# Block sums kept from the second normalisation, the search closed two units sooner, the bias kept on the chip, and low queries loaded once

## The chip, the cores and the metric

The kernel runs on one core of a Trainium2 chip. The metric is the device time of one execution in microseconds. The core has five engines that work side by side: TensorE (PE, matmuls, with its weight loads shown as PEld), VectorE (DVE), ScalarE (ACT), GpSimd (POOL) and SyncE (SP), which here only issues transfers (DMA). Each engine takes its instructions in one fixed order; a wait at the head of an engine's list holds everything behind it.

## The reference

One layer of an encoder on x of 2048 rows and 1024 columns, all in float32:

```python
xn = rms_norm(h, norm_gain[layer])
proj = xn @ w_in[layer]
qa, ka, va, ga, qb, kb, vb, gb, iq, ik, iw, za, zb = jnp.split(proj, offsets, axis=-1)
ya = chunked_relpos_attention(qa, ka, va, rel_bias[layer]) * jax.nn.silu(ga)
...
yb = dsa_sparse_attention(qb, kb, vb, iq, ik, iw) * jax.nn.silu(gb)
merged = sigmoid(za + b0) * (yA @ w_branch_a) + sigmoid(zb + b1) * (yB @ w_branch_b)
h = h + merged @ w_out[layer]
return rms_norm(h, final_norm_gain)
```

Branch A has 8 heads of 64; each chunk of 64 queries sees its own chunk and the 8 before, with a bias `rel_bias[h, clip(dist, -256, 256) + 256]`. For keys more than 256 rows back the distance is clipped, so the bias there is one number per head. Branch B scores all keys with an indexer (`iq`, `ik`, `iw`), takes the 256 best per query and attends to those.

## The kernel before

**Numbers.** A float32 operand is held as a high and a low part (`xh`, `xl`; weights likewise), both of the type fp32r; a product is three matmuls: high·high, high·low, low·high (`mm3`, L213). In the attention, `qs` holds the queries' high part on 128 rows (twice) and the low part on 128 rows (twice), and `kk` holds the keys' high part on rows 0–63 and low part on rows 64–127, so that two matmuls give all four products.

**Groups and slots.** x is cut into four groups g of 512 rows. Two slots of x are resident. First g=0 and 1 are projected; then `norm_again` (L1177) loads x of g=3 and 2 again, normalises and splits it (`split_x`: L225 on DVE, L226 on ACT, L227 on DVE) into the two slots.

**Jobs.** The projection is a list of jobs, each a unit of 256 columns by one group (two chunks of 24 matmuls 128x512; a `va` unit four chunks of 128x288). Jobs 0–39 do all units for g=0, 1. Jobs 40–43 are `va` for g=3 and 2, jobs 44–55 are the units of `rest` for g=3 and 2, in the order zb, za, qb. The other units of g=3 and 2 are done as 12 "quads": a Winograd scheme on 2x2 blocks, with 7 block products (84 matmuls) where 8 would be usual. Its inputs are the blocks A11, A12 (slot of one group, halves of the depth), A21, A22 and four block sums: A11 − A21 (stored over A21), S2, S1 and S4. `combine` (L1196) makes one sum for one k: POOL adds the high parts (L1203), DVE the low ones (L1204), DVE joins both (L1205), ACT rounds the high part (L1206), DVE takes the rest (L1207). It runs 16 times: four times behind the last g=3 job (`turned`), twelve times while the first quads run. The quads' weights come by `prep_full` (tiles `wst` from `wS`, combined on POOL at L1227–1233, split by L1236 and L1237).

**The search.** The top-k threshold search is written as generators that run between chunks: after each chunk `tick` lets DVE work worth `PUMP` or `PUMP2` be written. When all is written, `close_search` (L750) runs `search_again`: a matmul (L577) counts rows where the search failed, DVE turns the count into a flag (L579), and each engine passes a branch (for a slower search that isn't needed here). Behind the branch the search's buffers are given back, and the pools of the quads and of the attention are opened.

**The attention.** For each head and group, `load_a` (L835) loads `qs` (four transfers of 128 KB), `kk`, `vs` (the values, out of `vA`, in pieces of 512 B) and the bias tile of 640 columns, prepared for each head by `bias_half` (L659) during jobs 10–25. `a_unit` makes scores (L878) in two segments of 320 keys, or one where fewer than 640 are seen, and `softmax_piece` (L809) adds the bias.

The instructions are put in order by a scheduler when the program is built, so what follows what on an engine is read from the built program.

Of the kernel before, what the change touches and what calls it, by code (L numbers as in the profile page):

```python
# [8 lines left out]
F32 = mybir.dt.float32  # L9
# [31 lines left out]
PUMP, PUMP2 = 4500, 5400  # L41
# [12 lines left out]
CTB, WSB = 2, 5  # L54
# [38 lines left out]
def block_kernel(ctx: ExitStack, tc: tile.TileContext, io, dbg=None):  # L93
# [18 lines left out]
    vA = [scratch(f"vA{g}", [512, H, 2, HD]) for g in range(NG)]  # L112
# [11 lines left out]
    biasD = [scratch(f"biasD{h}", [128, 640]) for h in range(H)]  # L124
# [534 lines left out]
    def bias_half(j, gate):  # L659

        h, half = j // 2, j % 2
        c_ = slice(half * 320, half * 320 + 320)
        bt = ev.tile([128, 320], F32, name="bt", tag="ef")
        nc.gpsimd.tensor_copy(bt[:, 0:1], gate)
        nc.sync.dma_start(bt, io["bias"][h][:, c_])
        nc.gpsimd.tensor_scalar(bt, bt, -1.0, None, op0=OP.mult)
        if half:
            nc.gpsimd.memset(bt[0:64, 256:320], FAR)
        else:
            nc.gpsimd.memset(bt[64:128, 0:64], FAR)  # L670
        nc.sync.dma_start(biasD[h][:, c_], bt)
# [44 lines left out]
    def evac_v(c, g, o, acc):  # L716
        vv = ev.tile([128, 2, 32], F32R, name="vvt", tag="ef") if early_ else evl.tile([128, 2, 32], F32R, name="vv", tag="vv")
        nc.scalar.activation(vv[:, 0], acc[:, 256:288], AF.Copy)
        nc.vector.tensor_tensor(vv[:, 1], acc[:, 256:288], f32(vv[:, 0]), op=OP.subtract)  # L719
# [6 lines left out]
        nc.sync.dma_start(vA[g][o * 128:(o + 1) * 128, c * 4:c * 4 + 4], f32(e))  # L726
# [7 lines left out]
    rest = [u for k in ("zb", "za", "gb", "ga", "qb", "ka", "qa") for u in left[k]]  # L734
# [13 lines left out]
    dn = att = ldb = wp2 = ld = sml = wk = wy = wz = dna = wp_ = pl_ps = pe = psd = kBt = vBt = mk01 = None  # L748

    def close_search():  # L750

        nonlocal ld
        early_.append(1)
        stage.pop()
        search_again()
        search_st.close()
        ld = dph.enter_context(pool("ld", bufs=2, side="right"))

# [11 lines left out]
    def open_late():  # L770
        nonlocal dn, att, ldb, wp2, pl_ps, psd, kBt, vBt, mk01
        late.append(1)
        dn = dph.enter_context(pool("dn", bufs=2))
        att = ph.enter_context(pool("att"))
        ldb = ph.enter_context(pool("ldb", bufs=2))
        wp2 = ph.enter_context(pool("wp2"))
        pl_ps = dph.enter_context(pool("pl_ps", space=PSUM))
        psd = dph.enter_context(pool("psd", space=PSUM))
        kBt = att.tile([128, 2, S], F32R, name="kBt")
        vBt = att.tile([128, NT, 128], F32R, name="vBt")  # L780
        mk01 = att.tile([128, 2, 256], BF16, name="mk01")
# [53 lines left out]
    def load_a(G, h):  # L835
        base = max(0, 4 * G - 4)
        q = ld.tile([128, 2, 512], F32R, name="qs", tag="qs")
        for hl in range(2):
            for half in range(2):
                nc.sync.dma_start(f32(q[half * 64:half * 64 + 64, hl, :]), qA[G][hl, :, h, :])  # L840
        kk = ld.tile([128, 1024], F32R, name="kk", tag="kk")
        v = ld.tile([128, 8, 128], F32R, name="vs", tag="vs")
        for i, g in enumerate(range(max(0, G - 1), G + 1)):
            nc.sync.dma_start(f32(kk[:, i * 512:i * 512 + 512]), kA[g].rearrange("l r h n -> (l r) h n")[:, h, :])
            nc.sync.dma_start(f32(v[:, 4 * i:4 * i + 4]), vA[g][:, h].rearrange("(t p) l d -> p t (l d)", p=128))
        bias = ld.tile([128, 640], F32, name="bias", tag="bias")
        nc.sync.dma_start(bias, biasD[h])
        return base, q, kk, v, bias

    def a_unit(G, h):  # L850
        st = {}

        def loads():
            st["ld"] = load_a(G, h)
            if h % 2 == 0:
                sg = ld.tile([128, 512], F32, name="sg", tag="sg", bufs=SGB)
                nc.sync.dma_start(sg, gAD[G][(h // 2) * 128:(h // 2) * 128 + 128])
                shared["sg", "a", h // 2] = sg

        def one():  # L860
            base, q, kk, v, bias = st["ld"]
# [7 lines left out]
            for j in range(4):  # L869
                i = 4 * G + j  # L870
                f = max(0, i - 4)
                nk = (i - f + 1) * 128
                segs = [(0, 320), (320, 320)] if nk == 640 else [(0, nk)]
                for a, w in segs:
                    s_ps = next_s()
                    ko = (f - base) * 128 + a
                    for m in range(2):
                        nc.tensor.matmul(s_ps[:, :w], q[:, m, j * 128:(j + 1) * 128], kk[:, ko:ko + w],  # L878
                                         start=(m == 0), stop=(m == 1))
                    softmax_piece(s_ps[:, :w], bias[:, 640 - nk + a:640 - nk + a + w], a == 0,  # L880
                                  P[:, j, a:a + w], mx[:, j:j + 1])
                    yield
                nc.scalar.activation(P[:, j, :nk], P[:, j, :nk], AF.Exp, bias=mx[:, j:j + 1], scale=-1.0,  # L883
                                     accum_out=sm[:, h % 2, j:j + 1])

        def two():
            base, q, kk, v, bias = st["ld"]
# [257 lines left out]
    def attention():  # L1145
        units[1][0]()
# [49 lines left out]
    def combine(dst, a, b, op, k):  # L1196

        (ah, al), (bh, bl), (dh, dl) = a(k), b(k), dst(k)
        if early_:
            t, t2 = (mid.tile([128, 512], F32, name="ct", tag="wst", bufs=WSB) for _ in range(2))  # L1200
        else:
            t, t2 = (evl.tile([128, 512], F32, name="ct", tag="ct", bufs=CTB) for _ in range(2))
        nc.gpsimd.tensor_tensor(t, f32(ah), f32(bh), op=op)  # L1203
        nc.vector.tensor_tensor(t2, f32(al), f32(bl), op=op)  # L1204
        nc.vector.tensor_tensor(t, t, t2, op=OP.add)  # L1205
        nc.scalar.activation(dh, t, AF.Copy)  # L1206
        nc.vector.tensor_tensor(dl, t, f32(dh), op=OP.subtract)  # L1207
# [31 lines left out]
    for i, (how, r_, u, g) in enumerate(jobs):  # L1239
# [4 lines left out]
        for c in range(4 if kind == "va" else 2):  # L1244
            acc = next_acc(i)
            if kind == "va":
# [4 lines left out]
                for _ in range(1):  # L1251
                    if again:
                        again.pop(0)()
                tick(0.5)
            else:
# [23 lines left out]
    close_search()  # L1279
    mid_st = ExitStack()  # L1280
    mid = mid_st.enter_context(pool("mid", side="right"))
    sums_ = {n: [mid.tile([128, 4, 512], F32R, name=f"{n}{z}") for z in "hl"] for n in ("s4", "s1", "s2")}
# [29 lines left out]
    def rest_of(q):  # L1312
# [3 lines left out]
        for z, x_ in enumerate((S2, S1, S4)):  # L1316
# [7 lines left out]
    prep_full(0, "V")  # L1324
    prep_full(1)
    turns = [lambda k=k: combine(S2, A22, A21, OP.subtract, k) for k in range(4)]
    turns += [lambda k=k, f=f: f(k) for k in range(4) for f in (lambda k: combine(S1, S2, A11, OP.add, k),
                                                                lambda k: combine(S4, A12, S2, OP.subtract, k))]
    ahead = first(0)
    for _ in ahead:  # L1330
        turns.pop(0)()
    for q in range(nq):
# [4 lines left out]
        if turns:  # L1337
            for _ in nxt:
                while turns[:1]:
                    turns.pop(0)()  # L1340
# [149 lines left out]
```

## Time and profile before

| | |
|---|---|
| median of 3 runs | 2124.75 us (2120.24 to 2125.8) |
| profiled execution, device time | 2117.65 us |
| its span in the trace | 2115.9 us |
| granted PE clock, mean | 0.982 |
| PE busy | 2011.0 us (95%) |
| DVE busy | 1477.2 us (70%) |

The stages in the profiled execution, by their places in the trace: first norm and indexer to 120 us; jobs for g=0 and 1, with the search beside them, to about 610; normalising again and `va` to about 690; the `rest` jobs to 820; the quads to about 1096; the attention and the output projection to the end. A row of the table of stretches has the start and end, the length, then for PE, PEld, DVE, ACT and POOL the busy time and the instructions, then PE's granted clock (1.00 is full), the share of the DMA engines' time and GB/s. In a row of the timeline the bracket tells how long the engine stood before it, and what it waited for.

### The profile page before, as it was taken

The page shows a single profiled execution, that of the slowest core. Times are in us where ns is not written, and L with a number is a line of the kernel's source. Part 1 is how long each engine was busy: PE and PEld are TensorE (multiplying, and loading weights), DVE is VectorE, ACT ScalarE, POOL GpSimd, SP SyncE. Part 2 cuts the span into 40 slices and gives each one's busy share as a digit, 9 for nine tenths or more (in the row PEclk, how much of TensorE's full clock was granted, in tenths as well). Part 3 has the DMA queues.
Part 4 walks back from the last instruction along what each step waited for, and adds up shares of the span by engine and source line. Part 5 has one row for each costly group of instructions (what it writes and reads, how often), then busy time and mean ns, then how long its engine had stood idle before and what let it go on. Part 6 is the DMA issues. An engine that isn't in the chain of part 4 may idle for free.

```text
span 2115.9 us, 33695 instructions
## 1 busy us (share of the span) xinstructions
PE 2011.0 (95%) x10714; PEld 1699.1 (80%) x10714; DVE 1477.2 (70%) x3728; ACT 1264.9 (60%) x2590; POOL 777.5 (37%) x953
## 2 busy tenths in 40 slices
PE   8799999999989998799988999999999999999998
PEld 7578888889878886478766888888888888887886
DVE  5748887969789645966536677866886688875444
ACT  5456575555555623365437778967896688873221
POOL 2122223321131223655414556446444543442420
PEclk9899999999999999899999999999999999999999
DMA  9473344454463423234468766467445742145642
GB/s 358 140 227 128 122 154 154 133 197 133 160 207 97 149 88 128 70 106 144 130 206 246 215 198 195 138 190 235 119 136 175 228 130 63 60 132 181 217 144 90
DMA packets 236806, 334.29 MB, mean 158 GB/s; under 512 B 29264, under 2 KB 115664, under 8 KB 236496
## 3 DMA queue, kind: packets, MB, share of 16 engines
q1 hardware_dynamic: 236624, 332.10, 49.1%
q8 instruction: 85, 1.39, 0.3%
q14 instruction: 97, 0.79, 0.1%
HBM read 225.62 MB, written 106.40 MB: 157 GB/s over the span
## 4 chain that ended last, share of the span: by engine, by line
PE 46%; DMA 4%; DVE 4%; ACT 2%; issue 2%; POOL 1%; SPq 0%; DVEq 0%; ACTq 0%; POOLq 0%
PE acc L213 8%; PE po L1385 8%; PE d L213 7%; PE O L1013 5%; PE s L988 5%; PE pt L1005 5%; PE O L923 3%; PE s L878 2%; PE pt L913 2%; DMA dst<-wB 1%; DMA wst<-wS 1%; DVE P L809 1%; DMA dst<-wA 1%; DVE ct L1205 1%; DVE ct L1204 1%
## 5 line engine op out<-in xcount | busy, mean ns | idle before, releaser
L213 PE MATMUL acc<-xh,wt 128*128 128x512 f32 x1920 | 622.4, 396 | 16.9 <-ACT wt L1236 8.6
L213 PEld LDWEIGHTS acc<-xh,wt 128*128 128x128 f32 x1920 | 361.3, 189 | 102.5 <-ACT wt L1236 10.0
L213 PE MATMUL acc<-xl,wt 128*128 128x512 f32 x960 | 378.4, 394 | 0.0
L205 POOL TENSOR_TENSOR wt<-wst,wt 128x512 fp32r<-128x512 f32 (+1 forms) x116 | 149.5, 1317 | 406.3 <-ACT wt L204 376.9
L830 POOL TENSOR_TENSOR ptl<-pf,pth 128x512 fp32r<-128x512 f32 (+1 forms) x144 | 179.6, 1247 | 216.7 <-ACT pf L826 145.0
L833 DVE TENSOR_TENSOR ptl<-pt,pth 128x512 fp32r<-128x512 f32 (+1 forms) x288 | 187.3, 660 | 48.1 <-ACT pth L832 47.0
L213 PEld LDWEIGHTS acc<-xl,wt 128*128 128x128 f32 x960 | 181.7, 189 | 40.0
L482 DVE SCALAR_TENSOR_TENSOR sc<-lg,iw,sc 128x512 f32<-128x512 f32 (+2 forms) x266 | 179.1, 678 | 41.2 <-ACT lg L477 37.0
L477 ACT ACTIVATE lg<-lg 128x512 f32<-128x512 f32 (+2 forms) x304 | 150.2, 523 | 69.7 <-PE lg L475 68.0
L988 PE MATMUL s<-kBt,qsB 128*128 128x512 f32 (+3 forms) x640 | 187.7, 382 | 0.7 <-DVE mx L809 0.5
L832 ACT ACTIVATE pth<-pt 128x512 fp32r<-128x512 f32 (+1 forms) x288 | 160.9, 579 | 24.4 <-PE pt L1005 11.5
L1005 PE MATMUL pt<-ident,P 128*128 128x128 f32 x1088 | 165.6, 273 | 1.9 <-DVE ptl L833 0.8
L991 ACT ACTIVATE P<-P,mx 128x128 f32<-128x128 f32 (+15 forms) x128 | 154.6, 1209 | 15.4 <-DVE mx L809 14.8
L809 DVE CUSTOM_DVE_ANT_0 P<-s,mk,mx 128x512 f32<-128x512 f32 (+2 forms) x192 | 125.1, 652 | 35.3 <-PE s L988 29.2
L1013 PE MATMUL O<-pth,vBt 128*128 128x256 f32 x544 | 147.3, 289 | 2.0 <-DVE yb L1023 1.4
L1013 PE MATMUL O<-ptl,vBt 128*128 128x256 f32 x544 | 145.9, 295 | 1.6 <-POOL ptl L830 1.1
L1005 PEld LDWEIGHTS pt<-ident,P 128*128 128x128 f32 x1088 | 127.7, 140 | 10.9 <-ACT pf L826 2.1
L1051 POOL TENSOR_TENSOR dw<-dst,dw 128x512 fp32r<-128x512 f32 x64 | 83.3, 1301 | 126.6 <-ACT dw L1050 108.3
L878 PE MATMUL s<-kk,qs 128*128 128x320 f32 (+1 forms) x448 | 108.8, 338 | 15.3 <-DMA kk<-kA 9.3
L213 PE MATMUL acc<-wt,xh 128*128 128x288 f32 x512 | 107.6, 304 | 7.7 <-DVE vv L719 4.8
L988 PEld LDWEIGHTS s<-kBt,qsB 128*128 128x128 f32 x640 | 102.5, 189 | 13.8 <-DVE mx L809 6.6
L883 ACT ACTIVATE P<-P,mx 128x640 f32<-128x640 f32 (+4 forms) x128 | 98.0, 768 | 24.4 <-DVE mx L809 23.9
(287 smaller groups left out, 4603.3 us busy)
## 6 DMA issues: line engine op xcount, KB each, us to landing
wst<-wP SPq DMA_DIRECT2D x108, 256.0 KB
qs<-qA SPq DMA_DIRECT2D x128, 128.0 KB
kk<-kA SPq DMA_DIRECT2D x56, 256.0 KB
vs<-vA SPq DMA_DIRECT2D x56, 256.0 KB
wst<-wS SPq DMA_DIRECT2D x52, 256.0 KB
bias<-biasD SPq DMA_DIRECT2D x32, 320.0 KB
xrow<-x SPq DMA_DIRECT2D x16, 512.0 KB
sBD<-ef SPq DMA_DIRECT2D x32, 256.0 KB
```

The lines of the kernel that those rows point to most:

```text
L213: nc.tensor.matmul(acc, a, b, start=(first and i == 0), stop=(last and i == n - 1), **({} if first and last else {"skip_group_check": True}))
L477: nc.scalar.activation(lg, lg, AF.Relu)
L482: nc.vector.scalar_tensor_tensor(o_, lg, wv, o_, op0=OP.mult, op1=OP.add)
L830: nc.gpsimd.tensor_tensor(lo, pf, f32(hi), op=OP.subtract)
L832: nc.scalar.activation(hi, src, AF.Copy)
L833: nc.vector.tensor_tensor(lo, src, f32(hi), op=OP.subtract)
L878: nc.tensor.matmul(s_ps[:, :w], q[:, m, j * 128:(j + 1) * 128], kk[:, ko:ko + w], start=(m == 0), stop=(m == 1))
L988: nc.tensor.matmul(s_ps[:, :w], q[:, h, :], kBt[:, m, a:a + w], start=(m == 0), stop=(m == 1))
L991: nc.scalar.activation(P[:, e, :n], P[:, e, :n], AF.Exp, bias=mx[:, e:e + 1], scale=-1.0, accum_out=st["sum"][:, (u % 2) * 2 + e:(u % 2) * ...
L1005: nc.tensor.transpose(pt[:, k, e, :], P[:, e, (kt + k) * 128:(kt + k + 1) * 128], ident)
L1013: nc.tensor.matmul(o_, vBt[:, kt + k, :], src[:, k, :], start=(kt + k == 0 and n_ == 0), stop=(kt + k == b and n_ == 1), skip_group_check= ...
L1385: nc.tensor.matmul(accs[t, hf], a, b[:, n_], start=(k == 0 and i == 0), stop=(k == KT - 1 and i == 2))
```

## The change

1. **Block sums.** `norm_again` takes blocks k and k+4 together. For g=3 the normalised x is stored (`xnD`); for g=2 it is read back (`xa`), POOL makes all four sums in float32 with four operations, and two transfers store them (`sumD`). Later `load_sum` loads each sum and splits it with one ACT and one DVE operation. `combine` is gone. While such parts are pending, fewer are taken per chunk and `tick` is halved.
2. **The search's close.** `rest` begins with qb; `PUMP2` is 6900; `tick` itself calls `close_search` once the search is written. It opens three more accumulators (`psw`), and loads the sums.
3. **The bias.** `load_bias` loads 384 columns per head once (`bres`) and prepares them on POOL; five heads at the close, three when the attention opens. Beyond 384 keys the bias is a tile of zeros with the mask (`bfar`), as the constant of the head is taken off. Segments are 256 + 384 keys; 512 keys are 128 + 384.
4. **Low queries once.** `qs` takes three transfers instead of four, and the low part is multiplied on 64 rows (the product low·low is dropped).
5. **`vA`** is laid out so that a head's values for a group are one contiguous 2 KB row per partition; **`wst`** has 4 buffers instead of 5.

```diff
-PUMP, PUMP2 = 4500, 5400
+PUMP, PUMP2 = 4500, 6900
-CTB, WSB = 2, 5
+WSB, NB = 4, 5
...
-    def bias_half(j, gate):
-
-        h, half = j // 2, j % 2
-        c_ = slice(half * 320, half * 320 + 320)
-        bt = ev.tile([128, 320], F32, name="bt", tag="ef")
-        nc.gpsimd.tensor_copy(bt[:, 0:1], gate)
-        nc.sync.dma_start(bt, io["bias"][h][:, c_])
-        nc.gpsimd.tensor_scalar(bt, bt, -1.0, None, op0=OP.mult)
-        if half:
-            nc.gpsimd.memset(bt[0:64, 256:320], FAR)
-        else:
-            nc.gpsimd.memset(bt[64:128, 0:64], FAR)
-        nc.sync.dma_start(biasD[h][:, c_], bt)
+    def load_bias(heads, pl):
+
+        for h in heads:
+            bres[h] = pl.tile([128, 384], F32, name=f"bres{h}")
+            nc.sync.dma_start(bres[h], io["bias"][h][:, 256:640])
+        for h in heads:
+            c_ = pl.tile([128, 1], F32, name=f"bcol{h}")
+            nc.gpsimd.tensor_copy(c_, bres[h][:, 0:1])
+            nc.gpsimd.tensor_scalar(bres[h], bres[h], c_, -1.0, op0=OP.subtract, op1=OP.mult)
+            nc.gpsimd.memset(bres[h][0:64, 320:384], FAR)
...
-    rest = [u for k in ("zb", "za", "gb", "ga", "qb", "ka", "qa") for u in left[k]]
+    rest = [u for k in ("qb", "zb", "za", "gb", "ga", "ka", "qa") for u in left[k]]
...
     def close_search():
 
-        nonlocal ld
+        nonlocal ld, bfar, mid, psw, sums_
         early_.append(1)
-        stage.pop()
         search_again()
         search_st.close()
         ld = dph.enter_context(pool("ld", bufs=2, side="right"))
+        bp = dph.enter_context(pool("bp", side="right"))
+        bfar = bp.tile([128, 256], F32, name="bfar")
+        mid = mid_st.enter_context(pool("mid", side="right"))
+        psw = mid_st.enter_context(pool("psw", space=PSUM, side="right"))
+        sums_ = {n: [mid.tile([128, 4, 512], F32R, name=f"{n}{z}") for z in "hl"] for n in ("s1", "s2", "s4")}
+        stage[-1] = (mid, 4, WSB)
+        load_bias(range(NB), bp)
+        nc.gpsimd.memset(bfar, 0.0)
+        nc.gpsimd.memset(bfar[64:128, 0:64], FAR)
+        again.extend(lambda n=n, k=k: load_sum(n, k) for n in ("s2", "s1", "s4") for k in range(4))
+
+    def load_sum(n, k):
+
+        if n == "s3":
+            hi, lo = A21(k)
+        else:
+            hi, lo = (t[:, k] for t in sums_[n])
+        nc.sync.dma_start(f32(lo), sumD[("s3", "s1", "s2", "s4").index(n), k])
+        nc.scalar.activation(hi, f32(lo), AF.Copy)
+        nc.vector.tensor_tensor(lo, f32(lo), f32(hi), op=OP.subtract)
...
-        for hl in range(2):
-            for half in range(2):
-                nc.sync.dma_start(f32(q[half * 64:half * 64 + 64, hl, :]), qA[G][hl, :, h, :])
+        for hl, half in ((0, 0), (0, 1), (1, 0)):
+            nc.sync.dma_start(f32(q[half * 64:half * 64 + 64, hl, :]), qA[G][hl, :, h, :])
...
-                segs = [(0, 320), (320, 320)] if nk == 640 else [(0, nk)]
-                for a, w in segs:
+                segs = [(0, nk - 384, bfar[:, 640 - nk:256])] if nk > 384 else []
+                w = min(nk, 384)
+                segs.append((nk - w, w, bres[h][:, 384 - w:]))
+                for a, w, add in segs:
                     s_ps = next_s()
                     ko = (f - base) * 128 + a
-                    for m in range(2):
-                        nc.tensor.matmul(s_ps[:, :w], q[:, m, j * 128:(j + 1) * 128], kk[:, ko:ko + w],
+                    for m, r in ((0, 128), (1, 64)):
+                        nc.tensor.matmul(s_ps[:, :w], q[:r, m, j * 128:(j + 1) * 128], kk[:r, ko:ko + w],
                                          start=(m == 0), stop=(m == 1))
-                    softmax_piece(s_ps[:, :w], bias[:, 640 - nk + a:640 - nk + a + w], a == 0,
-                                  P[:, j, a:a + w], mx[:, j:j + 1])
+                    softmax_piece(s_ps[:, :w], add, a == 0, P[:, j, a:a + w], mx[:, j:j + 1])
...
+        elif not early_:
+            close_search()
...
-            nc.sync.dma_start(xs, io["xT"][g][:, k:k + 2, :])
+            nc.sync.dma_start(xs, io["xT"][g][:, k::4, :])
+            if g == 2:
+                xa = tkl.tile([128, 2, 512], F32, name="xa", tag="xa", bufs=1)
+                nc.sync.dma_start(xa, xnD[k])
             for z in range(2):
-                split_x(SLOT[g], k + z, xs[:, z], roots[g])
-
-        return [lambda k=k: part(k) for k in range(0, KT, 2)]
+                split_x(SLOT[g], k + 4 * z, xs[:, z], roots[g])
+            if g == 3:
+                nc.sync.dma_start(xnD[k], xs)
+                return
+            e = nc.gpsimd
+            e.tensor_tensor(xa[:, 1], xa[:, 1], xa[:, 0], op=OP.add)
+            e.tensor_tensor(xa[:, 0], xs[:, 0], xa[:, 0], op=OP.subtract)
+            e.tensor_tensor(xs[:, 0], xa[:, 1], xs[:, 0], op=OP.subtract)
+            e.tensor_tensor(xs[:, 1], xs[:, 1], xs[:, 0], op=OP.subtract)
+            for t, n in ((xa, 0), (xs, 2)):
+                nc.sync.dma_start(sumD[n:n + 2, k].rearrange("s p n -> p s n"), t)
+
+        return [lambda k=k: part(k) for k in range(4)]
 
     def next_acc(i=5):
-        n = rot("acc", 3 if i > 1 else 2)
-        return (psp, psp, psz)[n].tile([128, 512], F32, name="acc", tag=f"acc{n}")
+        n = rot("acc", 6 if early_ else 3 if i > 1 else 2)
+        return (psp, psp, psz, psw, psw, psw)[n].tile([128, 512], F32, name="acc", tag=f"acc{n}")
...
+                busy = bool(again)
+                if again and c % 2 == 0:
+                    again.pop(0)()
+                tick(0.25 if busy else 0.5)
...
+                busy = bool(again) and not early_
+                for _ in range(1 if busy and len(again) < 3 else 2):
                     if again:
                         again.pop(0)()
-                tick(1)
-        if i in range(BI0, BI0 + 16):
-            bias_half(i - BI0, f32(wt[:, 1, KT - 1, 255:256]))
+                tick(0.5 if busy else 1)
```

On PE, at the end of the search. Before, the closing matmul (`lg<-ones,bad`) stands behind all standard jobs, and the first products of the quads (accumulators 10065 and 10066, on the blocks `xh00` and `xh10` of the two slots) follow at once:

```order
L577 MATMUL lg_8079<-ones_148,bad_8076 1x1
L213 MATMUL acc_10065<-xh00_123,wt_7937 128x512
L213 MATMUL acc_10065<-xl00_124,wt_7937 128x512
...
L213 MATMUL acc_10066<-xh10_127,wt_7937 128x512
L213 MATMUL acc_10066<-xl10_128,wt_7937 128x512
...
L1478 UNCONDITIONAL_BRANCH
```

Now the chunks of the unit za stand behind it (accumulators 9912, 9734, 9768 and 9878, 24 matmuls each), and then the first quad (10046, 10047; 10105 takes the products with the sum S2):

```order
L578 MATMUL lg_7832<-ones_142,bad_7829 1x1
L214 MATMUL acc_9912<-xh00_117,wt_7663 128x512
...
L1493 UNCONDITIONAL_BRANCH
L214 MATMUL acc_9734<-xh10_121,wt_7663 128x512
...
L214 MATMUL acc_9768<-xh10_121,wt_7663 128x512
...
L214 MATMUL acc_9878<-xh00_117,wt_7663 128x512
...
L214 MATMUL acc_10046<-xh00_117,wt_9802 128x512
...
L214 MATMUL acc_10047<-xh10_121,wt_9802 128x512
...
L214 MATMUL acc_10105<-s2h_9698,wv_9803 128x512
```

Between the closing matmul and the first quad 96 matmuls have come to stand: 20 ahead of PE's branch and 76 behind it.

On SP, behind the same branch. Before, the weights of the quads (`wst<-wS`) come with little ahead of them:

```order
L1478 UNCONDITIONAL_BRANCH
L847 DMA bias<-biasD_98 128x640
L714 DMA qB_74<-eh 128x512
L714 DMA qB_74<-el 128x512
L857 DMA sg<-gAD_82 128x512
L847 DMA bias<-biasD_99 128x640
L1224 DMA wst<-wS 128x512 x3
```

Now the bias tiles and the block sums share the queue with them (`s2l`, `s1l`, `s4l` and `xl_122` are the low tiles into which a sum is loaded before it is split):

```order
L1493 UNCONDITIONAL_BRANCH
L664 DMA bres_9702<-bias 128x384
...
L664 DMA bres_9710<-bias 128x384
L775 DMA s2l<-sumD 128x512 x4
L1247 DMA wst<-wS 128x512
L775 DMA s1l<-sumD 128x512 x4
L775 DMA s4l<-sumD 128x512 x3
L1247 DMA wst<-wS 128x512
L775 DMA s4l<-sumD 128x512
L775 DMA xl_122<-sumD 128x512
L691 DMA sAD_93<-ef 128x512
L775 DMA xl_122<-sumD 128x512 x3
```

Two of the first quad's four weight tiles stand between the sums, the other two behind them.

On POOL, while x of g=2 is normalised. The weights of the two `va` units (`wt_5883`, `wt_6001`) are split there, and of the change the sums now stand among them, before none did:

```order
L206 TENSOR_TENSOR wt_5883<-wst_5896,wt_5883 128x4x128
L1216 TENSOR_TENSOR xs_6055<-xa_6057,xs_6055 128x512
L206 TENSOR_TENSOR wt_5883<-wst_5900,wt_5883 128x4x128
L1217 TENSOR_TENSOR xs_6055<-xs_6055 128x512
...
L206 TENSOR_TENSOR wt_6001<-wst_6018,wt_6001 128x4x128
L1217 TENSOR_TENSOR xs_6141<-xs_6141 128x512
L1214 TENSOR_TENSOR xa_6236<-xa_6236 128x512
L1215 TENSOR_TENSOR xa_6236<-xs_6234,xa_6236 128x512
```

One sum stands ahead of the last quarter of the first `va` weight, and the later ones follow each other without a weight between them.

More of the change, by code (lines that the diff above doesn't have):

```diff
@@ L111, in block_kernel @@
     kA = [scratch(f"kA{g}", [2, HD, H, 512]) for g in range(NG)]
-    vA = [scratch(f"vA{g}", [512, H, 2, HD]) for g in range(NG)]
+    vA = [scratch(f"vA{g}", [H, 128, 4, 2 * HD]) for g in range(NG)]
     qB = [scratch(f"qB{g}", [2, HD, H, 512]) for g in range(NG)]
@@ L123, in block_kernel @@
     sBD = [scratch(f"sBD{g}", [D, 512]) for g in range(NG)]
-    biasD = [scratch(f"biasD{h}", [128, 640]) for h in range(H)]
+    xnD = scratch("xnD", [4, 128, 2, 512])
+    sumD = scratch("sumD", [4, 4, 128, 512])
     tD = scratch("tD", [NG, 128, KT, 512])
@@ L725, in evac_v @@
         nc.vector.tensor_tensor(e[:, :, 1, :], v, f32(e[:, :, 0, :]), op=OP.subtract)
-        nc.sync.dma_start(vA[g][o * 128:(o + 1) * 128, c * 4:c * 4 + 4], f32(e))
+        nc.sync.dma_start(vA[g][c * 4:c * 4 + 4, :, o, :].rearrange("h p n -> p h n"), f32(e).rearrange("p h l d -> p h (l d)"))
     nu = len(UNITS)
@@ L747, in block_kernel @@
     ys, late = {}, []
-    dn = att = ldb = wp2 = ld = sml = wk = wy = wz = dna = wp_ = pl_ps = pe = psd = kBt = vBt = mk01 = None
+    dn = att = ldb = wp2 = ld = bfar = mid = psw = sums_ = sml = wk = wy = wz = dna = wp_ = pl_ps = pe = psd = kBt = vBt = mk01 = None
+    mid_st = ExitStack()
+    bres = {}
     def close_search():
-        nonlocal ld
+        nonlocal ld, bfar, mid, psw, sums_
         early_.append(1)
-        stage.pop()
         search_again()
@@ L781, in open_late @@
         mk01 = att.tile([128, 2, 256], BF16, name="mk01")
+        load_bias(range(NB, H), att)
         nc.vector.memset(mk01, 0.0)
@@ L844, in load_a @@
             nc.sync.dma_start(f32(kk[:, i * 512:i * 512 + 512]), kA[g].rearrange("l r h n -> (l r) h n")[:, h, :])
[L845 to L848, printed above, removed]
+            nc.sync.dma_start(f32(v[:, 4 * i:4 * i + 4]), vA[g][h])
+        return base, q, kk, v
     def a_unit(G, h):
@@ L853, in loads @@
         def loads():
-            st["ld"] = load_a(G, h)
-            if h % 2 == 0:
-                sg = ld.tile([128, 512], F32, name="sg", tag="sg", bufs=SGB)
+            if "ld" not in st:
+                st["ld"] = load_a(G, h)
+            if h % 2 == 0 and wz is not None:
+                sg = wz.tile([128, 512], F32, name="sg", tag="sg", bufs=SGB)
                 nc.sync.dma_start(sg, gAD[G][(h // 2) * 128:(h // 2) * 128 + 128])
@@ L860, in one @@
         def one():
-            base, q, kk, v, bias = st["ld"]
+            base, q, kk, v = st["ld"]
             P = next_p()
@@ L886, in two @@
         def two():
-            base, q, kk, v, bias = st["ld"]
+            base, q, kk, v = st["ld"]
             P = st["P"]
@@ L1145, in attention @@
     def attention():
+        units[0][0]()
         units[1][0]()
@@ L1194, in block_kernel @@
     A11, A12, A21, A22 = block(0, 0), block(0, 1), block(1, 0), block(1, 1)
[L1196 to L1207, printed above, removed]
     weights_ = {}
     def prep_full(q, what="WV"):
-        pl = mid if early_ else evl
+        pl = stage[-1][0]
         if "W" in what:
@@ L1250, in block_kernel @@
                 evac_v(c2, g, c, acc[:, :WT])
[L1251 to L1254, printed above, removed]
+                busy = bool(again)
+                if again and c % 2 == 0:
+                    again.pop(0)()
+                tick(0.25 if busy else 0.5)
             else:
@@ L1259, in block_kernel @@
                 evac(kind, c2 * 2 + c, g, acc)
-                for _ in range(2):
+                busy = bool(again) and not early_
+                for _ in range(1 if busy and len(again) < 3 else 2):
                     if again:
                         again.pop(0)()
-                tick(1)
-        if i in range(BI0, BI0 + 16):
-            bias_half(i - BI0, f32(wt[:, 1, KT - 1, 255:256]))
+                tick(0.5 if busy else 1)
         if (u, g) in ((b_, 0), (b_, 1)) and r_ < nu:
@@ L1268, in block_kernel @@
         if i == turned:
-            again += [lambda k=k: combine(A21, A11, A21, OP.subtract, k) for k in range(4)]
+            again[:0] = [lambda k=k: load_sum("s3", k) for k in range(4)]
         if i == turned:
-            prep_full(0, "W")
+            prep_full(0, "WV" if early_ else "W")
         for n in after.get(i, []):
@@ L1278, in block_kernel @@
         pump(1e9)
[L1279 to L1282, printed above, removed]
+    if not early_:
+        close_search()
+    for f in again:
+        f()
     def of_sum(n):
@@ L1323, in block_kernel @@
     nq = len(quads)
-    prep_full(0, "V")
+    if len(weights_[0]) == 4:
+        prep_full(0, "V")
     prep_full(1)
[L1326 to L1331, printed above, removed]
+    for _ in first(0):
+        pass
     for q in range(nq):
@@ L1336, in block_kernel @@
         nxt = first(q + 1) if q + 1 < nq else iter(())
[L1337 to L1340, printed above, removed]
         next(own)
```

## The prediction

> **What bounds the kernel now.** I read the page's first part, then the table of stretches, then the waits of PE in the stretches where PE isn't full.
>
> ```profile
> PE 2011.0 (95%) x10714; PEld 1699.1 (80%) x10714; DVE 1477.2 (70%) x3728; ACT 1264.9 (60%) x2590; POOL 777.5 (37%) x953
> 240.00:440.00 200.00, 200.00 (x878) 163.09 (x878) 167.39 (x420) 120.36 (x222) 63.57 (x81) 1.00 0.45 149
> 600.00:680.00 80.00, 69.04 (x428) 64.56 (x428) 75.14 (x171) 45.17 (x91) 20.56 (x15) 0.94 0.41 133
> 780.00:800.00 20.00, 20.00 (x88) 16.20 (x87) 1.32 (x4) 4.29 (x9) 5.33 (x10) 1.00 0.24 79
> 820.00:920.00 100.00, 73.52 (x264) 51.71 (x265) 82.08 (x135) 39.26 (x106) 59.92 (x90) 0.86 0.33 107
> 1080.00:1240.00 160.00, 137.67 (x801) 114.10 (x800) 99.03 (x306) 113.97 (x295) 65.39 (x71) 0.96 0.77 227
> 1240.00:1440.00 200.00, 196.79 (x1273) 173.84 (x1273) 144.90 (x409) 157.56 (x323) 105.18 (x101) 1.00 0.62 185
> ```
>
> Behind the stretch and its length stand PE's busy time and matmuls, then PEld, DVE, ACT, POOL, and the granted clock, DMA share and GB/s. PE bounds almost everything. Only three stretches of the changed part leave something: 600–680 (11.0 us idle, clock 0.94), 820–920 (26.5 idle, clock 0.86) and 1080–1240 (22.3 idle). At full rate, as in 780–800, a 128x512 matmul takes 20/88 = 0.227 us. The 264 matmuls of 820–920 are then 60 us of work, so that stretch **loses 40 us**, 13.5 of them to the clock.
>
> ```profile
> 798.67 2.58 DVE L1237 TENSOR_TENSOR wt<-wst,wt 128x256 fp32r<-128x256 f32 x5 [32.65 <-ACT wt L1236]
> 819.98 0.15 DVE L579 TENSOR_SCALAR flag<-lg 1x1 int32<-1x1 f32 x1
> 827.03 0.69 DVE L711 SCALAR_TENSOR_TENSOR el<-acc,eh 128x512 fp32r<-128x512 f32 x1 [6.90 <-issue]
> 829.81 1.36 SPq L1224 DMA_DIRECT2D wst<-wS  x3
> 832.65 0.31 ACT L1236 ACTIVATE wv<-wst 128x128 fp32r<-128x128 f32 x1 [9.14 <-DMA wst<-wS]
> 839.67 0.79 PE L213 MATMUL acc<-xh,wt 128*128 128x512 f32 x1 [8.15 <-ACT wt L1236]
> 860.00:880.00 20.00, 12.29 (x39) 8.10 (x38) 20.00 (x24) 4.54 (x8) 9.63 (x7) 0.75 0.11 40
> ```
>
> These rows show the entry to the quads. The search ended at 798.67 − 32.65 = 766.0, but the flag came only after the last standard job. DVE stands 6.9 us in the branch, SP issues the quad's weights behind it, and PE runs dry for 8.15 us. Then DVE, full in 860–880 with PE at 39 matmuls of 88, makes the sums:
>
> ```profile
> 879.34 1.66 POOL L1203 TENSOR_TENSOR ct<-s2h,xh 128x512 f32<-128x512 f32 x1 [1.83 <-DVE s4l L1207]
> 879.79 1.76 DVE L1204 TENSOR_TENSOR ct<-xl,s2l 128x512 f32<-128x512 f32 x1
> 882.68 0.68 DVE L1207 TENSOR_TENSOR s1l<-ct,s1h 128x512 fp32r<-128x512 f32 x1
> PE acc L213 <- DVE s1l L1207: 4.8, 3, 2.7
> ```
>
> A DVE add of 0.68 us takes 1.76 beside a POOL add: a POOL add costs DVE about 1.1 us.
>
> **Term 1, the entry to the quads: −28 us.** Now 96 matmuls of the last job (za) stand between the flag and the first quad: 20, then 72, then 4. That is 96 × 0.227 = 21.8 us of cover, where before PE came to the quad at once. Of the sums, 12 tiles with three DVE adds each become one DVE subtraction each; 24 DVE adds, 16.3 us alone and more beside POOL, leave the stretch that fills DVE. What is late next is DMA. Behind the branch (7 us, as above) SP issues 5 bias tiles of 196 KB, 16 sum tiles of 262 KB and the first quad's 4 weight tiles of 262 KB: 6.2 MB. The nearest rates of this trace bound the time:
>
> ```profile
> 820.00:840.00 20.00, 11.67 (x49) 9.06 (x50) 6.03 (x17) 5.36 (x18) 4.76 (x11) 0.89 0.60 193
> 1080.00:1100.00 20.00, 14.46 (x62) 10.82 (x60) 6.92 (x15) 3.26 (x6) 1.29 (x1) 0.96 0.90 277
> ```
>
> At 277 GB/s it is 22 us, at 193 it is 32, so the last tile lands 29 to 39 us behind the flag; PE finishes its cover at 22. The first weights and the S2 tiles (2.3 MB, 8 to 12 us) land in time, and the quad consumes the rest in the order of arrival while it has 84 × 0.227 = 19 us of work. So PE waits between 2 us and 17 (39 − 22), at a slow clock in between. I take 12 us lost, nearer to 277, the row with a queue as full as this one will be: 40 − 12 = 28. Bounds: 37 (3 lost) and 15 (17 and 8 of clock).
>
> The clock is weighed apart. The Trainium skill (TensorE: Matmul & The Clock Gate, "What's actually happening") says that the array falls to half clock after an idle window of about 3.4 us and recovers after as long a busy one. By that only the 8.15 us wait above would cost clock, an estimated 1.7 us, and my 12 would be about 10. The trace disagrees: the clock granted in 860–880 is 0.75 with no wait of 3.4 us there, so the rows stand.
>
> **Term 2, normalising again: +2 us.** 16 POOL ops are added, beside the last standard jobs:
>
> ```profile
> L1203 POOL TENSOR_TENSOR ct<-xh,xh 128x512 f32<-128x512 f32 x8 | 11.4, 1430 | 17.9 <-DVE ct L1205 7.8 <-DVE st L548 5.3 <-ACT xh L226 3.5
> L205 POOL TENSOR_TENSOR wt<-wst,wt 128x512 fp32r<-128x512 f32 x108 | 143.0, 1352 | 366.7 <-ACT wt L204 366.7
> 618.67 6.23 DVE L225 SCALAR_TENSOR_TENSOR xs<-xs,gcol,roots 128x512 f32<-128x512 f32 x4
> PE acc L213 <- DVE vv L719: 4.8, 1, 4.8
> 640.00:660.00 20.00, 20.00 (x147) 19.64 (x146) 18.03 (x61) 12.39 (x26) 0.00 (x0) 1.00 0.27 88
> ```
>
> They are 16 × 1.43 = 23 us of POOL, and up to 16 × 1.1 = 17 us of DVE. DVE was already short there (75.14 of 80; four L225 took 6.23 us, and PE waited 4.8 us for an evacuation behind them). Against it stand half the search work per chunk while parts are pending, and PE's idle 11.0 plus 0.06 × 80 = 4.8 of clock, which that can return in part. Two queues are passed: `xs` of the last g=2 part waits on SP for the store of part 1's sums, and one quarter of a va weight stands on POOL behind a sum (1.4 us). The 8 va chunks of g=3, 192 matmuls of 20/147 = 0.136 us, cover 26 us. The chain behind them is a load, four POOL ops (5.7), a store, a load and a split, where a transfer is 0.52 MB (2.7 us at the 193 GB/s above) and a split two L225 and four shorter ops (about 5): 8 + 6 + 2 × 5 = 24, just covered. Bounds −8 (half of the 16 lost) and +15 (17 of DVE uncovered, less what ticks free). I take +2.
>
> **Term 3, the start of the attention: −7 us.**
>
> ```profile
> PE s L878 <- DMA kk<-kA: 9.3, 4, 5.3
> DVE P L809 <- DMA bias<-biasD: 10.0, 4, 5.6
> DMA packets 22098, 23.93 MB, mean 239 GB/s; under 512 B 1666, under 2 KB 13795, under 8 KB 22089
> bias<-biasD SPq DMA_DIRECT2D x8, 320.0 KB
> qs<-qA SPq DMA_DIRECT2D x36, 128.0 KB
> ```
>
> Two waits and the transfers of 1080–1180. Its 8 bias tiles (2.6 MB) and a quarter of the `qs` (9 × 0.13 = 1.2 MB) go, three bias tiles (0.6) come: 3.2 MB at 239 GB/s is 13 us, the upper bound. Nothing is the lower, if the order of the queue rather than its bytes holds `kk`. PE's own wait for `kk` is 9.3, and part of it goes: 8. Against that, three POOL multiplications ahead of the first units cost 1 (L666, below, by 384/320 is 1.27 us each, mostly hidden). Later, in 1240–1440, PE has 3 us idle in 200, so there is nothing to win.
>
> **Edits at nothing.**
>
> ```profile
> L666 POOL TENSOR_SCALAR bt<-bt 128x320 f32<-128x320 f32 x16 | 16.9, 1055 | 28.5 <-DMA bt<-bias 28.5
> L878 PE MATMUL s<-kk,qs 128*128 128x320 f32 x384 | 91.4, 330 | 1.4 <-DVE mx L809 0.9
> ```
>
> The 16 bias halves lay at 241–431 us, where PE is 200.00 of 200 busy: free, and so is their absence. Segments of 256+384 have the columns of 320+320; 16 small matmuls more at G=0 are 16 × 0.06 = 1 us, in a stretch with idle PE. The low queries' 64 rows pass the same columns. No row shows 64 rows; bounds are nothing and, at half price for half of the x384, 192 × 0.227 × 320/512 / 2 = 14 us. I take nothing, as the nearest row is priced by columns. `vA` in 2 KB rows: same bytes, nothing.
>
> On the 64 rows the Trainium skill (TensorE: Matmul & The Clock Gate, "LDWEIGHTS") says that a weight load's time hangs on its columns and not its rows, which speaks against a gain; no run here shows it. By it the sum stays as it is.
>
> **Sum.** −28 + 2 − 7 = −33. The profiled run took 2117.65 (span 2115.9 and 1.75 around it), so 2085 for a like one. The three runs have the median 2124.75, 7.1 above it; on that scale the forecast is 2124.75 − 33 = **2092**.
>
> **Rivals.**
> 1. *The quads' entry becomes DMA-bound*: 6.2 MB at 193 GB/s, with the third weight tile behind the sums. Term 1 shrinks to 15, and DMA of 0.33 in that stretch speaks against it: 2105; with term 3 at nothing too, 2112.
> 2. *Normalising stalls*: term 2 at +15. For it: one `xa` buffer, stores waited for. Against: the 27 us of cover. 2105.
> 3. *Attention still waits for `kk`*: term 3 at +1, 2100.
> 4. *Slower: the search is late for its flag.* The closing matmul has moved 96 matmuls up, and PE now stands there until DVE is done.
>
> ```profile
> L475 PE MATMUL lg<-ikT,iqT x304: 277/392/502, 121.0 to 708.9; 128*128 128x512 f32 x100, 128*128 128x384 f32 x28, 128*128 128x256 f32 x24
> ```
>
> The tail from the last logits to the end was 766.0 − 708.9 = 57 us. In the changed order 324 matmuls stand between the same points: 324 × 0.227 = 73.6. Slack 16.6; each us of backlog beyond is a us of PE. It decides from 16.6 + 33 = 50 us of backlog; POOL's 17 and four qb chunks of six ops like L711's 0.69 (16) are 33 at most: 16 us lost, still faster. Only if va and qb evacuations also queue behind search steps (DVE was 35.33 busy of 60 in 710–770, so seldom) does it come to 55 + 16.6, giving 2124.75 − 33 + 55 = 2147.
>
> ```profile
> 710.00:770.00 60.00, 60.00 (x260) 48.63 (x259) 35.33 (x127) 28.22 (x41) 15.42 (x12) 1.00 0.35 116
> ```
>
> That the early close doesn't take place is ruled out by the order; it falls where it says.
>
> **Chances.** Forecast, within ±7: 0.51. Rival 1: 0.15. Rival 2: 0.15. Rival 3: 0.10. Rival 4: 0.09. 0.3%, or 6.4 us, is about what a measurement of this kernel can tell from no change. Rivals 1 and 2 together, or a part of 4, reach within it: 0.08. Slower 0.09, faster 0.83. The range: all three terms at their good ends are 37 + 8 + 13 = 58, or 2067, so I begin at 2068 (0.05 below, where the low rows' 14 would lie). Above, rivals 1 and 2 with term 3 at nothing are 2125; I stop at 2122 (0.13 above).
>
> **What would show it.** Right: the flag near 798, no DVE stretch of 20.00 with L1204/L1205, PE's loss in the 100 us behind the cover near 12; PE's idle of 1080–1240 down from 22.3 to 14; the stretch of the va jobs still near 428 matmuls in 80 us. Wrong: a wait of PE at L578 or at the first chunk behind it (rival 4); `PE acc <- DVE xl` or `ACT xh` at va g=2 of 5 us or more (rival 2); `wt <- wS` or `s1l`, `s4l` waits that add up to over 15 (rival 1); `kk` still at 9 us (rival 3).

## The result and the profile after

| | before | changed |
|---|---|---|
| median of 4 runs | 2123.24 us (2120.24 to 2125.8) | 2150.01 us (2146.35 to 2150.91) |
| ratio | | 1.0123, 95% interval 1.0104 to 1.0143 |
| span of the profiled execution | 2115.9 us | 2148.4 us |

The changed kernel is slower by 1.2%: 2150 us, where 2092 were forecast, 33 less than before. The page's first line and the same kinds of stretches, of the changed kernel (columns as before: PE, PEld, DVE, ACT, POOL, granted clock, DMA share, GB/s):

```profile
PE 2083.8 (97%) x10730; PEld 1713.9 (80%) x10730; DVE 1450.5 (68%) x3712; ACT 1273.2 (59%) x2590; POOL 774.5 (36%) x931
600.00:680.00 80.00, 67.13 (x428) 62.09 (x427) 77.55 (x177) 43.76 (x90) 38.32 (x29) 0.96 0.69 219
780.00:800.00 20.00, 20.00 (x89) 15.97 (x88) 0.15 (x1) 2.43 (x4) 0.50 (x1) 1.00 0.13 43
820.00:920.00 100.00, 97.38 (x410) 76.12 (x409) 62.66 (x139) 52.95 (x139) 55.96 (x110) 1.00 0.37 118
1240.00:1440.00 200.00, 199.36 (x1176) 163.40 (x1175) 136.40 (x376) 145.53 (x295) 94.76 (x91) 1.00 0.50 152
```

PE has 73 us more busy time than before with 16 instructions more. The entry to the quads (820–920) went from 264 matmuls to 410 at a full clock: there the forecast held. But 1240–1440, where nothing was expected, has 1176 matmuls instead of 1273, while PE looks *busier* (199.36 for 196.79 of 200). PE isn't waiting for another engine there; its own matmuls have become longer. (The two stretches stand 30 us apart in the work, as the attention begins earlier in the changed kernel. The run e1 below, in step with the changed kernel, has 1262 matmuls in the same stretch.)

Three marks split the span. They are the flag, the last addition of a quad (the last `part` operation) and the first matmul of the output projection (`po<-wos,mm`). Before:

```profile
L579 DVE TENSOR_SCALAR flag<-lg x1: 147/147/147, 820.0 to 820.0; 1x1 int32<-1x1 f32 x1
L1319 DVE TENSOR_TENSOR part<-acc,part x36: 673/683/692, 871.0 to 1096.0; 128x512 f32<-128x512 f32 x36
L1385 PE MATMUL po<-wos,mm x288: 390/396/503, 1921.2 to 2107.1; 128*128 128x512 f32 x144
```

and of the changed kernel (duration min/median/max in ns, then first and last start):

```profile
L580 DVE TENSOR_SCALAR flag<-lg x1: 148/148/148, 796.4 to 796.4; 1x1 int32<-1x1 f32 x1
L1341 DVE TENSOR_TENSOR part<-acc,part x36: 677/684/692, 845.5 to 1066.1; 128x512 f32<-128x512 f32 x36
L1400 PE MATMUL po<-wos,mm x288: 387/395/404, 1952.8 to 2139.9; 128*128 128x512 f32 x144
```

The quads end 29.9 us earlier (1096.0 to 1066.1). The attention behind them takes 886.7 us instead of 825.2: 61.5 us more. The whole loss, and more, lies in the attention.

The groups by shape, first of before, then of the changed kernel (busy us, then mean ns of one; some records are missing, so busy sums are low):

```profile
L878 PE MATMUL s<-kk,qs 128*128 128x320 f32 x384 | 91.4, 330 | 1.4 <-DVE mx L809 0.9
L878 PEld LDWEIGHTS s<-kk,qs 128*128 128x128 f32 x448 | 71.3, 194 | 23.5 <-DVE mx L809 11.9 <-issue 7.4 <-DVE ptl L833 1.6
```

```profile
L899 PE MATMUL s<-kk,qs 64*128 64x256 f32 x104 | 40.2, 387 | 0.0
L899 PE MATMUL s<-kk,qs 128*128 128x256 f32 x104 | 36.1, 347 | 0.2
L899 PEld LDWEIGHTS s<-kk,qs 64*128 64x128 f32 x232 | 44.1, 190 | 41.3 <-issue 28.5 <-DMA dst<-wB 0.3
```

A 64-row weight load itself is as long as a 128-row one (190 ns to 194), but 41.3 us of PEld's idle time stand before the 232 of them, 28.5 of it put down to no other engine. The timeline of the changed kernel shows it in one place, PE first, then PEld:

```profile
1268.70 0.79 PE L899 MATMUL s<-kk,qs 128*128 128x384 f32 x2
1269.41 0.44 PE L943 MATMUL O<-ptl,vs 128*128 128x384 f32 x1
```

```profile
1268.67 0.19 PEld L899 LDWEIGHTS s<-kk,qs 128*128 128x128 f32 x1
1269.05 0.18 PEld L899 LDWEIGHTS s<-kk,qs 64*128 64x128 f32 x1 [0.18 <-issue]
1269.41 0.19 PEld L943 LDWEIGHTS O<-ptl,vs 128*128 128x128 f32 x1 [0.18 <-issue]
```

The 64-row load starts 0.35 us after the pair's first matmul, when that matmul's columns are through (a 128x384 matmul whose weights are ready shows 0.33 to 0.34 us a little earlier in this trace), and the next 128-row load (for `O`) starts only when the 64-row matmul is through. In between PE has no weights ready. Elsewhere loads run beside the matmul ahead. The matmul behind such a late load is shown from its load's start on (1269.41 in both views), and so PE looks busy. That suggested theory A: a change between 128 and 64 rows, in both directions, makes the weight load wait. Theory B: the other edits to the attention (segments of 256+384, resident bias, order of the transfers) slow it.

### The profile page after: what moved, and what is told of

Its sections match the earlier page's. It is cut to its first block, busy times and chain, and to the rows that moved or that the text cites. A ratio compares the mean times of both kernels' runs of the same rounds, so it can differ in the third digit from the quotient of the medians.

```text
span 2148.4 us, 33517 instructions
## 1 busy us (share of the span) xinstructions
PE 2083.8 (97%) x10730; PEld 1713.9 (80%) x10730; DVE 1450.5 (68%) x3712; ACT 1273.2 (59%) x2590; POOL 774.5 (36%) x931
## 4 chain that ended last, share of the span: by engine, by line
PE 74%; DMA 11%; DVE 5%; POOL 4%; issue 3%; ACT 2%; SPq 1%; another core or an unknown queue 0%; DVEq 0%; POOLq 0%; ACTq 0%
PE acc L214 27%; PE d L214 8%; PE O L1033 6%; PE po L1400 6%; PE s L899 6%; PE s L1008 6%; PE pt L1025 6%; DMA wst<-wS 4%; PE O L943 4%; PE pt L933 3%; PE lg L476 3%; DMA mf<-mD 1%; POOL wst L1255 1%; DMA xrow<-x 1%; DMA wst<-wP 1%
## 5 line engine op out<-in xcount | busy, mean ns | idle before, releaser
L899 PE MATMUL s<-kk,qs 128*128 128x256 f32 (+2 forms) x464 | 165.4, 397 | 6.8 <-DVE mx L830 5.4
L899 PEld LDWEIGHTS s<-kk,qs 128*128 128x128 f32 x464 | 90.2, 194 | 58.3 <-issue 33.0
```

The lines of the kernel that those rows point to most:

```text
L899: nc.tensor.matmul(s_ps[:, :w], q[:r, m, j * 128:(j + 1) * 128], kk[:r, ko:ko + w], start=(m == 0), stop=(m == 1))
```

## The experiments

All ratios are to runs of the kernel before on the same chip. Between the sets of runs the median of the kernel before moves by up to 3 us (2120.37 to 2123.24), so where two medians of different sets are compared, the difference by the ratios stands beside it.

**The low product on 128 rows again (e1).** Only part 4 is undone:

```diff
-        for hl, half in ((0, 0), (0, 1), (1, 0)):
+        for hl, half in ((0, 0), (0, 1), (1, 0), (1, 1)):
...
-                    for m, r in ((0, 128), (1, 64)):
+                    for m, r in ((0, 128), (1, 128)):
```

> The changed kernel with part 4 undone: four qs transfers, the low product on 128 rows again. Theory A (the 64-row weight loads can't be hidden behind the matmul ahead, nor the next 128-row load behind the 64-row matmul): the attention's 61 us come back, about 2150 - 61 = 2089 us, and pairs of L899 take what columns cost (256 columns: near 0.5 us shown for a pair instead of 0.68). Theory B (the 256+384 segments, the resident bias or the transfers' new order slow the attention): stays near 2150.

2087.59 us, ratio 0.9841 (0.9819 to 0.9863). That is 62.4 us less than the changed kernel (60 by the ratios), as theory A has it. The marks, the pairs and the stretch of this run:

```profile
L1341 DVE TENSOR_TENSOR part<-acc,part x36: 676/684/692, 846.9 to 1066.1; 128x512 f32<-128x512 f32 x36
L1400 PE MATMUL po<-wos,mm x288: 387/395/404, 1892.5 to 2079.3; 128*128 128x512 f32 x144
1256.67 0.48 PE L899 MATMUL s<-kk,qs 128*128 128x256 f32 x2
1256.99 0.63 PE L214 MATMUL d<-yb,dw 128*128 128x512 f32 x2
1256.64 0.30 PEld L899 LDWEIGHTS s<-kk,qs 128*128 128x128 f32 x2
1240.00:1440.00 200.00, 195.82 (x1262) 173.25 (x1261) 144.12 (x397) 154.51 (x311) 104.88 (x99) 1.00 0.59 178
```

The quads end at the same 1066.1; the attention takes 826.4 us. A pair of 256 columns shows 0.48 us, where the timeline of the changed kernel has

```profile
1270.75 0.68 PE L899 MATMUL s<-kk,qs 128*128 128x256 f32 x2
1271.36 0.73 PE L214 MATMUL d<-yb,dw 128*128 128x512 f32 x2
```

and the two weight loads run into each other (0.30 us for both). These durations overlap with the next row's. From start to start a pair takes 0.32 us here and 0.61 in the changed kernel, 0.29 more. Theory B falls: segments, resident bias and all the rest of the change are in this run.

The single loads of the traces show both directions. Taken are the pairs whose two loads and the next load stand side by side (198 in the changed kernel, 213 in e1). PEld's idle time before the pair's second load adds up to 35.2 us in the changed kernel and 1.2 in e1; before the load behind the pair it is 29.4 against 9.9. So the way in adds about 34 us and the way out about 20. For all 232 pairs that would be some 63 us, so the fourth transfer that e1 brings back isn't needed to explain the 62.

**The kernel before with part 4 alone (e2).**

```diff
-        for hl in range(2):
-            for half in range(2):
-                nc.sync.dma_start(f32(q[half * 64:half * 64 + 64, hl, :]), qA[G][hl, :, h, :])
+        for hl, half in ((0, 0), (0, 1), (1, 0)):
+            nc.sync.dma_start(f32(q[half * 64:half * 64 + 64, hl, :]), qA[G][hl, :, h, :])
...
-                    for m in range(2):
-                        nc.tensor.matmul(s_ps[:, :w], q[:, m, j * 128:(j + 1) * 128], kk[:, ko:ko + w],
+                    for m, r in ((0, 128), (1, 64)):
+                        nc.tensor.matmul(s_ps[:, :w], q[:r, m, j * 128:(j + 1) * 128], kk[:r, ko:ko + w],
```

> The kernel before with part 4 alone (three qs transfers, low product on 64 rows; 224 pairs of 320 columns or one segment). Theory A: 224/232 of 61 us, about 59 us slower, 2182. Theory B: as before, 2123, or a few us faster for the transfers saved.

2188.72 us, ratio 1.0322 (1.0282 to 1.0361): 68 us slower, 0.30 us for each of 224 pairs and 9 more than expected; the changed kernel's own price is 62.4/232 = 0.27. The edit alone does the damage, with a quarter of the `qs` transfers saved.

**Is it each 64-row load, or the switch? (e5, control e6.)** The low matmul is cut into two halves of its columns, each with a weight load of its own; e5 on 64 rows in the changed kernel, e6 on 128 rows in e1:

```diff
-                    for m, r in ((0, 128), (1, 64)):
+                    for m, r, c, n in ((0, 128, 0, w), (1, 64, 0, w // 2), (1, 64, w // 2, w - w // 2)):
```

> The changed kernel with each 64-row low matmul cut into two halves of its columns, so that two 64-row weight loads follow each other (232 more matmuls and loads). If only the switch between 128 and 64 rows holds a load up, the added matmul costs its own small pitch, 10 to 20 us against the control e6's own increase. If every 64-row load waits for the matmul ahead, each added one costs about half of what a pair now loses (61/232/2 = 0.13 us): 30 us or more beyond the control's increase.

> Control for the split: e1 with its low matmul cut into two column halves at 128 rows, 232 more matmuls and loads that can be hidden. Theory A: at most the pitch of a small matmul each, 232 x 0.06 = 14 us over e1; it may be less, as a weight load of 0.19 us then covers more of them.

e5 took 2168.46 us, ratio 1.022 (1.0196 to 1.0243), 18.5 over the changed kernel (20.6 by the ratios); e6 2109.82, ratio 0.9946 (0.993 to 0.9961), 22.2 over e1. Adding 232 loads costs no more on 64 rows than on 128: a 64-row load behind a 64-row matmul isn't held up. e5's weight loads show it:

```profile
1263.27 0.29 PEld L899 LDWEIGHTS s<-kk,qs 64*128 64x128 f32 x2 [0.25 <-issue]
1263.63 0.20 PEld L933 LDWEIGHTS pt<-ident,P 128*128 128x128 f32 x2
```

Idle before the first of the two, then both in 0.29 us, one beside the other. Counted as above, PEld's idle time in e5 is 35.2 us before the first 64-row load, 0.7 before the second and 17.0 before the 128-row load behind them; in e6 it is 1.0, 0.0 and 5.7. So the price is the switch between row counts, in both directions. The two 64-row loads of e5 bring the same weights; different ones were not tried. e6 cost more than the 14 us it was given; a small matmul's pitch is not all of what an added pair of load and matmul takes.

**The early close (e4).** e1 with `tick` no longer closing the search:

```diff
-        elif not early_:
-            close_search()
```

> e1 (128 rows) with the early close taken out: the search closes behind all standard jobs, as before the change, and the 16 sums are read back there. If the 96 matmuls of cover carry term 1, the sums and weights (about 5.2 MB, 19 us at 277 GB/s behind a branch of 7 us) come with PE idle: 15 to 25 us slower than e1, about 2105 to 2113. If the gain came from the sums alone (POOL and DVE relieved), it stays within 6 us of e1's 2088.

2101.77 us, ratio 0.991 (0.988 to 0.9939), 14.2 slower than e1. The entry of this run:

```profile
820.00:840.00 20.00, 11.19 (x50) 8.93 (x48) 9.38 (x15) 9.65 (x17) 11.20 (x19) 0.89 0.78 261
840.00:860.00 20.00, 17.68 (x59) 12.61 (x60) 15.17 (x36) 10.68 (x34) 15.47 (x30) 0.77 0.41 123
860.00:880.00 20.00, 20.00 (x88) 16.32 (x88) 14.86 (x33) 10.55 (x32) 13.57 (x28) 1.00 0.38 129
PE acc L214 <- ACT wv L1257: 10.8, 2, 9.5
L1339 DVE TENSOR_TENSOR part<-acc,part x36: 676/683/692, 849.0 to 1076.9; 128x512 f32<-128x512 f32 x36
```

PE waits 9.5 us at once for weights of the quad behind the flag and is full again at 860, where before it stayed short to 920. The quads end at 1096.0 before, 1076.9 here and 1066.1 with the early close. So the gain at the entry has two parts: 19 us come without the early close, above all with the sums that DVE no longer makes there (what the other edits at this place add, such as the three accumulators, was not tried apart), and 11 (14 by the medians, just under the 15 to 25 expected) by the cover of the early close.

**The bias as before (e7, and again as e10 beside a repeat of e1, e9).** e1 with `bias_half`, a bias tile per unit and segments of 320+320:

```diff
-                segs = [(0, nk - 384, bfar[:, 640 - nk:256])] if nk > 384 else []
-                w = min(nk, 384)
-                segs.append((nk - w, w, bres[h][:, 384 - w:]))
-                for a, w, add in segs:
+                segs = [(0, 320), (320, 320)] if nk == 640 else [(0, nk)]
+                for a, w in segs:
+                    add = bias[:, 640 - nk + a:640 - nk + a + w]
```

> e1 (128 rows) with the bias as before the change: prepared in 16 halves, loaded per unit (320 KB), segments 320+320. If the resident bias wins at the attention's start (term 3 as forecast, 13 us of transfers at most), this is 4 to 10 us slower than e1, about 2092 to 2098. If the start is held by something else, it is within 3 us of e1.

> The kernel of e1 again, as the measure for the two runs beside it: 2088 within 4 us.

> The kernel of e7 again on the same chip as e1's: if the resident bias is worth what the attention's length showed (839 us without it, 826 with it) less the 5.6 us it costs at the entry, 4 to 7 us slower than e9; if that was chance, within 3 us.

e7 took 2093.81 us, ratio 0.9861 (0.9833 to 0.9889); e10 2088.87, ratio 0.9859 (0.9838 to 0.9879), beside e9 with 2088.93, ratio 0.9848 (0.983 to 0.9867). e7 lies within the 4 to 10 us that were expected, e10 isn't slower than e9, and the intervals lie over each other: the resident bias is worth nothing that shows. By the marks it is a trade. In e10 the quads end at 1058.0, in e9 at 1065.8; the attention takes 833.3 us in e10 and 826.0 in e9. What the resident bias saves in the attention (7.3) it loses ahead of it (7.8): 2.4 are there at the flag (795.5 in e10, 797.9 in e9), and 5.4 come between the flag and the end of the quads, where five tiles stand ahead of the sums.

**The bias tiles later (e8).** e1 with the five tiles loaded when the third quad's weights are made, behind a copy from a late tile:

```diff
-        load_bias(range(NB), bp)
+        bias_later.append(lambda gate: load_bias(range(NB), bp, gate))
...
+        if q == 3:
+            bias_later.pop()(f32(weights_[2][3][1][:, 3, 0:1]))
```

> e1 (128 rows) with the five resident bias tiles loaded and prepared when the third quad's weights are made, no longer ahead of the sums at the search's close. In e7, without any bias there, the quads ended at 1060.5 us and in e1 at 1066.1. If that difference is the bias tiles' place ahead of the sums and weights, the quads end near 1061 and the run is 3 to 6 us faster than e1, about 2083. If it is chance between executions, the same as e1 within 3 us.

2084.22 us, ratio 0.9845 (0.9824 to 0.9867). In its trace the quads end at 1061.4, 4.4 us before e9's, and the attention takes 824.2. By the medians it is 4.7 us below e9, as expected; but the ratios differ by 0.0003 (e9 has 0.9848), and the runs can't tell the two apart. Both beat the kernel before and the changed one.

## Why the prediction was wrong

**The step that failed** is "the low queries' 64 rows pass the same columns … I take nothing, as the nearest row is priced by columns". Its bounds were nothing and a gain of 14 us; the measured price is a loss of 62 (changed kernel to e1) to 68 us (e2). A loss was left out of the bounds with equal columns as the reason, and that was no reason: columns price the matmul and the load one by one, and the loss is in their overlap. Every row of the trace of before has 128 rows by 128 columns for these loads, and none has a switch; a bound for the unseen shape was to be had from those rows: one unhidden load (0.19 us) on the way in and one on the way out of 224 pairs, 85 us. The rule of the Trainium skill that stood beside it (TensorE: Matmul & The Clock Gate, "LDWEIGHTS") holds for the load's length, 190 ns to 194, and says nothing of when it may start.

**Rivals.** None was this. The slower one, a search late for its flag, didn't come: the flag is at 796.4, as foretold near 798, and PE reached it without a wait.

**Term 1, −28, and term 2, +2**, were right in their sum: the quads end 29.9 us earlier, where 26 were forecast. The flag came at 796.4, about 2 us ahead of 820.0 less the 21.8 of cover; as it lies between 795.5 and 800.3 in the eight kernels with the early close, term 2 can't be told from nothing. PE's idle in 820–920 is 2.6 us. The 600–680 stretch has 428 matmuls, as before, with DVE at 77.55 and POOL at 38.32 for 20.56: the 16 sums found their cover. The waits there have other names, but the same size:

```profile
PE acc L214 <- DVE sm L547: 4.7, 1, 4.7
PE acc L214 <- DVE vv L717: 3.4, 1, 3.4
```

The late transfers that were forecast as the new limit show as one short hole: 69 matmuls in 820–840.

```profile
800.00:820.00 20.00, 20.00 (x88) 16.06 (x86) 11.11 (x18) 10.64 (x22) 15.65 (x24) 1.00 0.92 324
820.00:840.00 20.00, 18.18 (x69) 12.34 (x69) 19.81 (x39) 12.79 (x39) 18.39 (x35) 1.00 0.40 119
```

19 matmuls are missing there, 4 us; over 820–920 it is 30 of 440, 6.8 us, where 12 were forecast. (The forecast's lower bound for this wait is 2 us in one sentence and 3 in the sum, and neither comes out of the landing times, which give 29 − 22 = 7; rival 2 has 27 us of cover, where the working gives 26. Nothing hangs on either.) The transfers behind the flag came at 324 GB/s, more than the 277 taken.

**Term 3, −7**, was wrong by itself. With 128 rows the attention takes 826.4 us in e1 and 826.0 in e9, where it took 825.2 before: nothing was gained, as in rival 3. Its first 160 us behind the quads are alike, before and in e1:

```profile
1096.00:1256.00 160.00, 139.35 (x842) 117.88 (x843) 105.80 (x334) 125.11 (x320) 74.63 (x80) 0.96 0.75 221
1066.00:1226.00 160.00, 138.57 (x844) 118.55 (x843) 105.15 (x341) 121.63 (x313) 76.99 (x86) 0.96 0.68 200
```

DMA fell from 221 to 200 GB/s and PE did not gain. PE's wait for `kk` fell from 9.3 to 3.5 us, but 4.0 for `qs` came in its place, and that for the softmax's `mx` stayed (4.9, now 5.5). The attention with the old bias (e10, 833.3) is longer than that of the kernel before, though the quads ahead of it end earlier. The difference lies at its start: e10 has 799 matmuls in 1060–1220, where e9 has 843 in 1066–1226. What holds it there stays open.

So without part 4 the sum comes out: −33 was forecast, and e1 is 32.9 us below the kernel before of its own chip (2120.47). That it fits so closely is luck in part. The two profiled executions are 28.1 us apart: 29.9 less to the end of the quads, 1.2 more in the attention and 0.6 more in the output projection. The larger gain at the entry (4 us) makes up half of the miss in term 3 (8); the rest of the fit is in the spread of the executions.

**What the profile could not show.** The rows that priced columns were right, and the shape was new. A busy PE hides this loss: nothing in the list of PE's waits names it. It shows in PEld, in idle time before loads that is put down to "issue":

```profile
PEld s L899 <- issue: 22.7, 113, 0.3
```

is the top row of PEld's waits in 1240–1840 of the changed kernel, 113 times at most 0.3 us; e1 has no such row for L899 among its first.

## What to carry to other kernels

Mixing matmuls of different row counts in a dense stream took 0.27 to 0.30 us per pair here, more than the transfers it saved; keep the row count and pay for the duplicate transfer, unless the small ones can stand together (two 64-row loads in a row overlapped; no run here made a gain of it). An edit that "passes the same columns" is not free by that: ask what the weight load beside it overlaps with. And when a stage is bound by PE, compare the count of matmuls per stretch, not PE's busy share, which rose here while the work per us fell.

## What the runs showed of the hardware

- The weight load of a matmul on 64 rows did not run beside a matmul on 128 rows, and the load for 128 rows behind it was late too: 62 us over 232 pairs, while 64 behind 64 overlapped (idle of 0.7 us before the second of them in e5, of 35.2 before the first). Only fp32r operands and these two row counts, both from row 0 on, were run.
- In the changed kernel the granted clock stayed low at the attention's start while PE showed no idle time:

```profile
1080.00:1100.00 20.00, 20.00 (x83) 14.32 (x82) 11.38 (x43) 14.13 (x40) 6.23 (x9) 0.76 0.41 120
```

  PE is 20.00 of 20 busy at a clock of 0.76. In e1, whose quads end at the same 1066.1, this stretch has a clock of 0.91, with PE busy for 14.42. The wait ahead is not the reason by itself, as both kernels have it (5.44 us in the changed kernel, 5.47 in e1). In e5 the clock is 0.50 in this stretch and 0.72 in the next, with PE 20.00 of 20 busy in both; in its control e6 it is 0.81 and 0.91. So in these traces, one execution of each kernel, it goes with the 64-row matmuls; why stays open.
